# Two query and key jobs of a retention layer ahead of the layer norm that feeds them

## Chip, cores and metric

One core of a Trainium2 chip. The metric is the device time of one execution in microseconds (us). Five engines take part: TensorE (PE, matrix products; PEld in the profile is its weight load), VectorE (DVE), ScalarE (ACT), GpSimd (POOL) and SyncE (SP, which here only issues loads).

## What is computed

Two transformer blocks over 256 positions of 2048 values. The place of the change is the passage from the first layer of the second block (attention, then a layer norm) to its second layer (retention):

```python
def layer_norm(x, gain, bias):
    x32 = x.astype(jnp.float32)
    mu = jnp.mean(x32, axis=-1, keepdims=True)
    var = jnp.mean(jnp.square(x32 - mu), axis=-1, keepdims=True)
    y = (x32 - mu) * lax.rsqrt(var + LN_EPS)
    return (y * gain.astype(jnp.float32) + bias.astype(jnp.float32)).astype(x.dtype)
...
def retention_mixer(h, w_in, decay_exp, w_out, cos, sin):
    B, S, _ = h.shape
    proj = h @ w_in
    q, k, v, g = jnp.split(proj, [R_QK_WIDTH, 2 * R_QK_WIDTH, 2 * R_QK_WIDTH + R_V_WIDTH], axis=-1)
    q = apply_rope(q.reshape(B, S, R_HEADS, R_QK_DIM), cos, sin)
    k = apply_rope(k.reshape(B, S, R_HEADS, R_QK_DIM), cos, sin) * (R_QK_DIM ** -0.5)
...
def second_block(x, attn_w_in, ...):
    ...
        x = layer_norm(ALPHA * x + y, ln_gain[i], ln_bias[i])
```

So with s = ALPHA·x + (attention output), the retention layer multiplies norm(s) by its weights. There are 8 heads of 256 query and key values and 512 values.

## The kernel before

All activations are kept transposed: 16 tiles of 128 features by 256 positions, each as a pair of a rounded part (hi, columns 0 to 255) and what the rounding left (lo, columns 256 to 511). A weight unit of 128x1024 values is loaded by SP as `wf`, rounded by ACT to `wh` (L375), and DVE makes the rest, `wl` = `wf` − `wh` (L388). A product is wh·[hi lo] (512 columns, L450) plus wl·hi (256 columns, L451): a pair. Jobs whose result is not transposed use three 512-wide matmuls (L473 to L475). `next_unit` asks for `wh` three units ahead and for `wl` two units ahead, four buffers of each; a unit lasts 8 pairs.

The order of jobs is written by `plan()`, and all matmuls stand on PE in that order. Everything else is written as Python generators, which `Sched` moves on by one step each time that the matmuls written so far make another 650 ns (`S.adv(325)` per pair); a generator's `yield n` leaves n such steps. Each engine works through its own queue in the order written. So a vector operation stands in its engine's queue between the weight splits where the generator put it, and a split written behind an operation that waits, waits with it.

Stage d ends with four jobs ao (`mm` = 0 to 3), 64 pairs each: the attention output projection, four tiles of 128 features a job. The last two weight units of each job are taken together, tile by tile (`tail=2`), so that the tiles of a job end 8 matmuls apart. `ev_res` adds a finished tile (the hi and lo halves of its PSUM bank, L1375 and L1377) to `xr[k]`, which holds ALPHA·x. The class `LN` gathers the statistics meanwhile: the sum of the first 8 tiles, `lnc`, gives a preliminary mean; once mm=1 has ended, `shift` subtracts it from all 16 tiles (L1296), and `stat` makes a square on ACT (L1320) and two running sums on POOL (L1321, L1323). In mm=3 the weights' last two units come from extra buffers (`alt`), and its 512-wide matmuls are written as two 256-wide ones (`one`, L447 and L448), so that the lo part doesn't need a column of its own to add up. Sums over features are one-column matmuls with a vector of ones (L1342); tiles 14 and 15 have their own. `finish` computes mean and 1/sigma by 13 small DVE operations (L1349 to L499), spreads both over the partitions by two matmuls with diagonals (`lpb` L1358, `lpn` L1366), and `apply0` makes the 16 normed tiles `x3` (named xB): scaling on POOL (L1642), shift on DVE (L1643), gain and bias on ACT (L1646) and on POOL or ACT (L1648, L1650), lo part on DVE (L1654).

Stage e reads `x3`: rqk(0) (query and key of head 0, four tiles, 64 pairs), rv(0) (values), rqk(1,0), rqk(1,2), rv(1), and so on. `task_rope(h)` rotates query and key of a head (L1752 to L1771); rope(0) begins when rqk(0) has ended. `decay` computes the retention decays in 16-column operations on DVE and a logarithm on ACT, during mm=1.

Of the kernel before, what the change touches and what calls it, by code (L numbers as in the profile page):

```python
# [18 lines left out]
P = 128  # L19
# [17 lines left out]
def plan():  # L37
# [72 lines left out]
    for h in range(8):  # L110
        if h == 0:
            job("e", "T", allk, rt(256 * h) + rt(2048 + 256 * h), 2, ("rqk", h, 0))
        else:
            job("e", "T", allk, rt(256 * h), 4, ("rqk", h, 0))
            job("e", "T", allk, rt(2048 + 256 * h), 4, ("rqk", h, 2))
        job("e", "N", allk, [(w, 4096 + 512 * h + ar(512))], 2, ("rv", h))
# [219 lines left out]
def body(tc, a, out, stop=None, dbg=None):  # L336
# [26 lines left out]
    def prefetch(to, alt=None):  # L363

        to = min(len(us), to)
        while pos["sp"] < to:
# [3 lines left out]
            if not raw:  # L370
                if alt is None:
                    wh[q] = pw.tile([P, 1024], F32R, name="wh", tag="wh", bufs=4)
                else:
                    wh[q] = alt.tile([P, 1024], F32R, name="wh", tag="wh", bufs=2)
                ACT.activation(wh[q][:, :n], wf[q][:, :n], AF.Copy)  # L375
            pos["sp"] += 1
        low(to if alt else to - LAG, alt)

    def low(to, alt=None):
        while pos["lo"] < to:  # L380
            q = pos["lo"]
            st, o, n, raw = us[q]
            if not raw:
                if alt is None:
                    wl[q] = pw.tile([P, 1024], F32R, name="wl", tag="wl", bufs=4)
                else:
                    wl[q] = alt.tile([P, 1024], F32R, name="wl", tag="wl", bufs=2)
# [4 lines left out]
    def next_unit(hold=False, alt=None):  # L392
        u = pos["u"]
        if alt is not None:
            low(pos["sp"])
            prefetch(u + SA + 1, alt)
        elif not hold:
# [19 lines left out]
    def job_T(j, xs, evac, tail=1, alt=None, raw=None, one=False):  # L417
# [6 lines left out]
        for c in range(nch - tail + 1):  # L424
            w, ks = {}, []
            for cc in range(c, nch if c == nch - tail else c + 1):
                k0 = cc * kc
                kn = min(kc, K - k0)
                h, l = next_unit(tail > 1 and cc == nch - 1, alt if tail > 1 and cc >= nch - 2 else None)
# [10 lines left out]
            for n, (m, kk) in enumerate(order):  # L440
# [4 lines left out]
                cs = slice(m * P, m * P + P)  # L445
                if one:
# [791 lines left out]

    x2 = XS(S)
    for h in range(2):  # L1240
        act = XS(S, HFF)
        while jq[0]["tag"][0] == "gu":
# [15 lines left out]
    class LN:  # L1258
        tag = "m"

        def __init__(self, pool, x, pair):
# [4 lines left out]
            self.task = None  # L1266
            self.x, self.pair = x, pair
# [20 lines left out]

        def shift(self):
# [3 lines left out]
            ACT.activation(self.c, pb[:, :T], AF.Copy, scale=1.0 / (8 * P))  # L1293
# [75 lines left out]
    def ev_res(ln, mm):  # L1369
        def f(m, p):  # L1370
            k = 4 * mm + m
            S.drain(ln.tpre)
            if k >= 8:
                S.drain(ln.task)
# [581 lines left out]
```

## Time and profile before

| | us |
|---|---|
| median of 3 runs (2297.22 to 2302.93) | 2300.92 |
| the profiled execution | 2303.65 |
| its span in the profile | 2301.9 |
| PE busy in the span | 2265.1 |
| DVE, ACT, POOL busy in the span | 1522.9, 1126.2, 396.2 |
| mm=3 of ao, first to last matmul | 31.41 |
| end of ao to the first matmul of rqk(0) | 9.08 |

The span runs from the first to the last instruction that the profiler saw; the execution's own time has what lies around it as well. PE is busy all the time but for a few places, so the time line of those places, the wait that ended last there, and the granted clock of the stretch are what to read. A granted clock of 1.00 is TensorE's upper level, 2.4 GHz, 0.50 its lower one, 1.2 GHz.

### The profile page before, as it was taken

What the parts mean: (1) busy time and instruction counts of PE and PEld (TensorE: products, weight loads), DVE (VectorE), ACT (ScalarE), POOL (GpSimd) and SP (SyncE); (2) the same over time, 40 slices, a digit from 0 to 9 for tenths busy, and PEclk for the clock granted to TensorE, in tenths of its full rate; (3) what the DMA queues carried; (4) which work ended last, traced back from release to release, by engine and by line L of the source; (5) the groups of instructions that cost most, each with busy time, mean ns of one, the idle gap of its engine ahead of it and who ended that gap; (6) DMA issues with size and microseconds to landing.
All of it is one profiled execution on the core that took longest, in us unless ns stands there. A gap on an engine that the chain in (4) does not pass through costs nothing.

```text
span 2301.9 us, 32643 instructions
## 1 busy us (share of the span) xinstructions
PE 2265.1 (98%) x12407; PEld 1949.7 (85%) x12407; DVE 1522.9 (66%) x2334; ACT 1126.2 (49%) x1642; POOL 396.2 (17%) x369
## 2 busy tenths in 40 slices
PE   8999999999999999999999999999999999999998
PEld 7977878888888888888888888888888888888886
DVE  6666697755555555555558898777676676766554
ACT  5457545554443444454445556454444544445442
POOL 2224341111110011110012222650000000001120
PEclk9999999999999999999999999989999999999998
DMA  7643355566665566656565454444555655556553
GB/s 246 233 147 119 111 186 189 183 192 192 192 193 191 181 191 191 194 188 193 191 191 175 150 157 152 156 166 161 185 169 174 186 165 183 168 173 217 188 182 119
DMA packets 113757, 409.82 MB, mean 178 GB/s; under 512 B 12816, under 2 KB 13072, under 8 KB 113342
## 3 DMA queue, kind: packets, MB, share of 16 engines
q1 hardware_dynamic: 111456, 399.75, 54.2%
q0 software_dynamic: 1424, 6.86, 0.9%
q8 instruction: 97, 1.59, 0.3%
q10 hardware_dynamic: 720, 1.13, 0.1%
q14 instruction: 60, 0.49, 0.1%
HBM read 405.57 MB, written 4.21 MB: 178 GB/s over the span
## 4 chain that ended last, share of the span: by engine, by line
PE 83%; DVE 6%; POOL 2%; issue 1%; ACT 1%; DMA 0%; DVEq 0%; POOLq 0%; ACTq 0%
PE st L450 37%; PE st L451 19%; PE st L473 7%; PE st L474 7%; PE st L475 7%; DVE wl L388 2%; PE mO L1808 1%; POOL xr L1296 1%; PE mA L853 1%; PE mS L1781 0%; PE st L1924 0%; POOL lny L1648 0%; PE mO L834 0%; POOL xr L1642 0%; PE mT L1826 0%
## 5 line engine op out<-in xcount | busy, mean ns | idle before, releaser
L388 DVE TENSOR_TENSOR wl<-wf,wh 128x1024 fp32r<-128x1024 f32 (+1 forms) x750 | 953.2, 1280 | 300.7 <-ACT wh L375 299.4
L375 ACT ACTIVATE wh<-wf 128x1024 fp32r<-128x1024 f32 (+1 forms) x750 | 789.5, 1055 | 696.8 <-PE st L450 397.3
L450 PE MATMUL st<-xA,wh 128*128 128x512 f32 x1952 | 690.4, 397 | 8.0 <-DVE xA L513 6.8
L451 PE MATMUL st<-xA,wl 128*128 128x256 f32 x2016 | 567.8, 282 | 2.6 <-DVE wl L388 2.6
L450 PE MATMUL st<-xB,wh 128*128 128x512 f32 x1536 | 548.8, 401 | 6.0 <-DVE evs L662 2.8
L450 PEld LDWEIGHTS st<-xA,wh 128*128 128x128 f32 x1952 | 367.5, 188 | 89.2 <-DVE xA L513 6.8
L451 PE MATMUL st<-xB,wl 128*128 128x256 f32 x1536 | 432.6, 282 | 0.0
L451 PEld LDWEIGHTS st<-xA,wl 128*128 128x128 f32 x2016 | 384.3, 191 | 3.8 <-DVE wl L388 3.6
L450 PEld LDWEIGHTS st<-xB,wh 128*128 128x128 f32 x1536 | 290.5, 189 | 76.3 <-DVE xB L1654 4.3
L451 PEld LDWEIGHTS st<-xB,wl 128*128 128x128 f32 x1536 | 292.3, 190 | 1.1
L450 PE MATMUL st<-act,wh 128*128 128x512 f32 x704 | 244.1, 392 | 0.0
L451 PE MATMUL st<-act,wl 128*128 128x256 f32 x704 | 197.4, 280 | 0.0
L474 PE MATMUL st<-wl,xB 128*128 128x512 f32 x448 | 175.0, 391 | 1.1 <-DVE wl L388 1.1
L473 PE MATMUL st<-wh,xB 128*128 128x512 f32 x448 | 175.5, 392 | 0.0
L475 PE MATMUL st<-wh,xB 128*128 128x512 f32 x448 | 174.7, 390 | 0.0
L450 PEld LDWEIGHTS st<-act,wh 128*128 128x128 f32 x704 | 131.8, 187 | 28.5
L662 DVE TENSOR_TENSOR evs<-st,evt 128x256 f32<-128x256 f32 x110 | 46.1, 423 | 144.1 <-ACT evt L660 143.8
L451 PEld LDWEIGHTS st<-act,wl 128*128 128x128 f32 x704 | 133.4, 189 | 0.0
L473 PE MATMUL st<-wh,xA 128*128 128x512 f32 (+2 forms) x320 | 122.7, 384 | 0.0
L474 PE MATMUL st<-wl,xA 128*128 128x512 f32 (+2 forms) x320 | 118.5, 370 | 0.5 <-DVE wl L388 0.5
L475 PE MATMUL st<-wh,xA 128*128 128x512 f32 (+2 forms) x320 | 118.4, 370 | 0.0
L1209 POOL TENSOR_TENSOR evs<-evs,R 128x256 f32<-128x256 f32 x44 | 32.4, 737 | 476.8 <-DVE evs L662 476.8
(444 smaller groups left out, 2509.3 us busy)
## 6 DMA issues: line engine op xcount, KB each, us to landing
wf<-in_w_c SPq DMA_DIRECT2D x264, 512.0 KB, 4.2
wf<-in_w_e SPq DMA_DIRECT2D x256, 512.0 KB, 3.7
wf<-in_w_d SPq DMA_DIRECT2D x112, 512.0 KB, 3.7
wf<-in_w_a SPq DMA_DIRECT2D x84, 512.0 KB, 3.6
wf<-in_w_b SPq DMA_DIRECT2D x32, 512.0 KB, 4.1
xr<-in_xT SPq DMA_DIRECT2D x16, 256.0 KB, 5.7
wf<-in_w_a SPq DMA_DIRECT2D x5, 420.0 KB, 4.2
dr<-d POOLq DMA_DIRECT2D x1, 2048.0 KB, 9.7
```

The lines of the kernel that those rows point to most:

```text
L375: ACT.activation(wh[q][:, :n], wf[q][:, :n], AF.Copy)
L388: V.tensor_tensor(wl[q][:, :n], wf[q][:, :n], wh[q][:, :n].bitcast(F32), OP.subtract)
L450: PE.matmul(ps[m], hv[:, cs], x, start=kk == 0, stop=False)
L451: PE.matmul(ps[m][:, :T], lv[:, cs], x[:, :T], start=False, stop=kk == K - 1)
L473: PE.matmul(p, xh, h[:, o:o + n], start=kk == 0, stop=False)
L474: PE.matmul(p, xh, l[:, o:o + n], start=False, stop=False)
L475: PE.matmul(p, xl, h[:, o:o + n], start=False, stop=kk == K - 1)
L662: V.tensor_tensor(s, p[:, :T], t, OP.add)
L853: PE.matmul(pv[:, y, :], qT[i // 2][64 * g:64 * g + 64, i % 2, tt * P:tt * P + P], kT[64 * g:64 * g + 64, b, 0:W], start=True, stop=True)
L1209: G.tensor_tensor(s, s, R2, OP.mult)
L1296: (V if k % 3 == 2 else G).tensor_tensor(xr[k], xr[k], self.c, OP.subtract)
L1808: PE.matmul(po, l[:, st_, o], r_[:, st_], start=i == 0, stop=i == 5)
```

## The change

The norm is linear in s but for its two numbers per position, r = 1/sigma and c = −mean/sigma: norm(s)·W = r·(W·(g s)) + c·(W·g) + W·b, with gain g and bias b. The first two jobs behind ao, rqk(0) and now rqk(1,0), which is moved ahead of rv(0), read new tiles `xg`: the hi and lo parts of g·s without the norm, and four columns between them that hold gain and bias (each hi and lo). Their triples (260, 256, 258 columns) so give W·(g s), W·g and W·b at once, and `ev_first` applies r and c to the finished tiles. `xg` is made by `gain` as soon as the statistics of a tile are written. The norm's sums and broadcasts (`norm0`) are steps of the scheduler among these jobs, `apply0` follows them, and all later jobs read `x3` as before. The preliminary mean comes from the first 4 tiles (`NS`), its subtraction begins with mm=1. The special forms of mm=3 (`alt`, `one`) are not used there, tiles 14 and 15 go through the running sums. The opening of the next stage's pools, the load of the rotation's table and rope(0) go to a function, `phase4`, called when the first half of rv(0) has ended; rope(h) follows rope(h−1). `decay` runs in the second half of the first block's FFN.

```diff
@@ plan
+            if h > 1:
+                job("e", "T", allk, rt(256 * h), 4, ("rqk", h, 0))
             job("e", "T", allk, rt(2048 + 256 * h), 4, ("rqk", h, 2))
+        if h == 0:
+            job("e", "T", allk, rt(256), 4, ("rqk", 1, 0))
@@ job_T
+                if ext:
+                    PE.matmul(ps[m][:, :T + 4], hv[:, cs], x[:, :T + 4], start=kk == 0, stop=False)
+                    PE.matmul(ps[m][:, :T], hv[:, cs], x[:, T + 4:2 * T + 4], start=False, stop=False)
+                    PE.matmul(ps[m][:, :T + 2], lv[:, cs], x[:, :T + 2], start=False, stop=kk == K - 1)
+                    if kk == K - 1:
+                        evac(m, ps[m])
+                    S.adv(340)
+                    continue
@@ LN
+        NS = 4
...
         def shift(self):
-            yield 6
+            yield 5
...
-            for k in [*range(8, 16), *range(8)]:
-                (V if k % 3 == 2 else G).tensor_tensor(xr[k], xr[k], self.c, OP.subtract)
-                if k < 8:
+            n = 0
+            for k in [*range(self.NS, 16), *range(self.NS)]:
+                (V if n % 3 == 2 else G).tensor_tensor(xr[k], xr[k], self.c, OP.subtract)
+                n += 1
+                yield 1
+                if k < self.NS:
+                    S.add(self.stat(k))
                     yield 2
-                    yield from self.stat(k)
...
         def stat(self, k):
+            yield 2
...
+            elif k < 14 or self.done:
                 sq = self.base.tile([P, T], F32, name="lnt", tag="lnt", bufs=3)
                 ACT.activation(sq, xr[k], AF.Square)
                 G.tensor_tensor(self.s, self.s, xr[k], OP.add)
                 yield 1
                 (G if k < 12 else V).tensor_tensor(self.q, self.q, sq, OP.add)
...
+            if self.done:
+                yield 1
+                yield from self.done(k)
@@ finish
+            yield 1
             rsqrt(r[:, 0:2], v, None, None, 2)
+            yield 1
...
                 if z == 2:
+                    if self.done:
+                        yield 2
                     PE.matmul(pb[:, :T], ones, dg[:, :T], start=True, stop=True)
...
+            if self.done:
+                yield 2
             pn = self.pp.tile([P, 512], F32, name="lpn", tag=self.tag)
@@ new: the un-normed tiles, the norm among the jobs
+    def gain(k):
+
+        x = q3.tile([P, 528], F32R, name="xg", tag=f"xg{k}")
+        g = lng[0][:, k:k + 1]
+        ACT.activation(x[:, :T], xr[k], AF.Copy, scale=g)
+        G.tensor_copy(x[:, T:T + 4], cgb[:, k])
+        yield 2
+        V.scalar_tensor_tensor(x[:, T + 4:2 * T + 4], xr[k], g, x[:, :T].bitcast(F32), OP.mult, OP.subtract)
+        xg.t[k] = x
+
+    def gain_by(k):
+        xg.by[k] = S.add(gain(k))
+        if k == 15:
+            tap.append(S.add(norm0()))
+            tap.append(S.add(apply0()))
+        yield 1
...
+    def norm0():
+
+        yield 4
+        ln0.head()
+        ln0.sums(ln0.s, ln0.q, True)
         yield 1
+        yield from ln0.finish()
@@ apply0
+        yield tap[0]
+        rm = ln0.rm
...
-            yield 1 if k < 8 else 2
-
-    tap = S.add(apply0())
+            yield 2 + (k % 3 > 0)
+
+    ln0.begin()
+    for mm in range(1, 4):
+        job_T(take(), og, ev_res(ln0, mm), 2)
...
@@ the jobs' results
+    def ev_first(h, m, p):
+
+        w, s = m // 2, m % 2
+        if s == 0:
+            qkr[(h, w)] = xa_tile("qkr", (P, 2, T))
+        S.drain(tap[0])
+        gb = small(2)
+        V.tensor_reduce(gb, p[:, T:T + 4].rearrange("p (a b) -> p b a", a=2), AX.X, OP.add)
+        q = qkr[(h, w)][:, s]
+        V.tensor_tensor(q, p[:, :T], ln0.rm[1], OP.mult)
+        V.scalar_tensor_tensor(q, ln0.rm[2], gb[:, 0:1], q, OP.mult, OP.add)
+        ACT.activation(q, q, AF.Identity, bias=gb[:, 1:2])
...
+    for h in range(2):
+        job_T(take(), xg, lambda m, p: ev_first(h, m, p), ext=True)
...
+            if (h, tt) == (0, 0):
+                phase4()
```

PE's queue at the end of ao, before: sums between the last pairs, the two broadcasts (`lpb`, `lpn`), then rqk(0) on normed tiles (xB); `pcs` is the PSUM bank of the sums.

```order
L451 MATMUL st<-xA,wl 128x256
L1342 MATMUL pcs<-ones,lns 128x1 x2
L1342 MATMUL pcs<-ones,lnq 128x1 x2
L447 MATMUL st<-xA,wh 128x256
L448 MATMUL st<-xA,wh 128x256
L451 MATMUL st<-xA,wl 128x256
L1342 MATMUL pcs<-ones,xr 128x1 x2
L1342 MATMUL pcs<-ones,lnu 128x1 x2
L1342 MATMUL pcs<-ones,xr 128x1 x2
L1342 MATMUL pcs<-ones,lnu 128x1 x2
L1358 MATMUL lpb<-lndg,ones 128x256
L1366 MATMUL lpn<-lndg,ones 128x256
```

The same place of PE's queue after the change: the last of the nine triples between ao's last pair and the sums, the sums, and the first triple of the ten that stand ahead of `lpb`.

```order
L441 MATMUL st<-xg,wh 128x260
L442 MATMUL st<-xg,wh 128x256
L443 MATMUL st<-xg,wl 128x258
L1359 MATMUL pcs<-deps,ones 128x1 x2
L1393 MATMUL pcs<-ones,lns 128x1 x2
L1393 MATMUL pcs<-ones,lnq 128x1 x2
L441 MATMUL st<-xg,wh 128x260
L442 MATMUL st<-xg,wh 128x256
L443 MATMUL st<-xg,wl 128x258
```

Nothing of the norm is ahead of the first triple any more; nine triples are ahead of the sums, ten more ahead of `lpb`, and three more ahead of `lpn`.

DVE's queue there, before, from the last weight splits of ao to the norm's first small operation (the numbers behind the names tell buffers apart).

```order
L388 TENSOR_TENSOR wl_14528<-wf_14408,wh_14526 128x1024
L388 TENSOR_TENSOR wl_14534<-wf_14438,wh_14532 128x1024
L1375 TENSOR_TENSOR xr_13733<-st_14329,xr_13733 128x256
L1323 TENSOR_TENSOR lnq_13542<-lnq_13542,lnt_14554 128x256
L1375 TENSOR_TENSOR xr_13733<-st_14330,xr_13733 128x256
L1323 TENSOR_TENSOR lnq_13542<-lnq_13542,lnt_14571 128x256
L1375 TENSOR_TENSOR xr_13761<-st_14331,xr_13761 128x256
L1375 TENSOR_TENSOR xr_13761<-st_14332,xr_13761 128x256
L1349 TENSOR_SCALAR sm_14614<-pcs_14356 128x2
```

DVE's queue there after the change; `xg` is the lo part of an un-normed tile (L1651), L385 a weight split.

```order
L1434 TENSOR_TENSOR xr_13808<-st_14364,xr_13808 128x256
L1651 SCALAR_TENSOR_TENSOR xg_14574<-xr_13780,vec_72,xg_14574 128x256
L1372 TENSOR_TENSOR lnq_13589<-lnq_13589,lnt_14581 128x256
L1372 TENSOR_TENSOR lnq_13589<-lnq_13589,lnt_14586 128x256
L1651 SCALAR_TENSOR_TENSOR xg_14589<-xr_13780,vec_72,xg_14589 128x256
L385 TENSOR_TENSOR wl_14605<-wf_14438,wh_14522 128x1024
L385 TENSOR_TENSOR wl_14607<-wf_14460,wh_14601 128x1024
L1651 SCALAR_TENSOR_TENSOR xg_14594<-xr_13808,vec_72,xg_14594 128x256
L1651 SCALAR_TENSOR_TENSOR xg_14614<-xr_13808,vec_72,xg_14614 128x256
L385 TENSOR_TENSOR wl_14642<-wf_14482,wh_14603 128x1024
L1400 TENSOR_SCALAR sm_14662<-pcs_14649 128x2
```

The first job's second and third weight units (wl_14605, wl_14607) are now split behind the last tile's additions, its statistics and one or two `xg` parts. Before, the first job's second and third units (wl_14528, wl_14534) were split ahead of the last four tiles' additions.

## Rows read from the trace of the kernel before

**Rows 1.** Page, sections 1 (busy) and 5 (costliest groups): busy, mean ns, idle before.

```profile
PE 2265.1 (98%) x12407; PEld 1949.7 (85%) x12407; DVE 1522.9 (66%) x2334; ACT 1126.2 (49%) x1642; POOL 396.2 (17%) x369
...
L375 ACT ACTIVATE wh<-wf 128x1024 fp32r<-128x1024 f32 (+1 forms) x750 | 789.5, 1055 | 696.8 <-PE st L450 397.3
```

**Rows 2.** Windows: length, busy of PE, PEld, DVE, ACT, POOL, granted clock, DMA.

```profile
900.00:970.00 70.00, 70.00 (x406) 61.83 (x405) 39.75 (x51) 34.87 (x52) 10.88 (x14) 1.00 0.60 187
...
1483.72:1515.13 31.41, 27.53 (x207) 26.84 (x205) 18.71 (x22) 13.82 (x21) 18.86 (x20) 0.89 0.56 185
...
1493.26:1499.82 6.56, 5.61 (x24) 5.31 (x25) 6.56 (x4) 3.09 (x4) 6.56 (x5) 0.50 0.45 142
...
1515.13:1524.21 9.08, 3.92 (x22) 2.93 (x21) 5.55 (x23) 3.69 (x7) 2.48 (x4) 0.60 0.01 2
...
1516.89:1527.13 10.24, 5.08 (x14) 3.42 (x13) 6.53 (x24) 4.41 (x8) 5.40 (x8) 0.50 0.01 2
...
1524.21:1560.00 35.79, 34.84 (x173) 28.77 (x174) 30.30 (x48) 23.93 (x39) 22.13 (x23) 0.96 0.44 148
```

**Rows 3.** Time line, norm and rqk(0): start, length, engine, line, operation, [idle <-releaser].

```profile
1513.88 0.50 PE L1342 MATMUL pcs<-ones,lns 128*128 128x1 f32 x4
...
1517.01 0.16 DVE L1349 TENSOR_SCALAR sm<-pcs 128x2 f32<-128x2 f32 x1 [1.25 <-PE pcs L1342]
...
1520.01 1.22 PE L1358 MATMUL lpb<-lndg,ones 128*128 128x256 f32 x2 [3.04 <-ACT lndg L1361]
...
1524.21 0.80 PE L450 MATMUL st<-xB,wh 128*128 128x512 f32 x1 [2.12 <-DVE xB L1654]
...
1528.10 0.28 PE L451 MATMUL st<-xB,wl 128*128 128x256 f32 x1
...
1531.28 0.28 PE L451 MATMUL st<-xB,wl 128*128 128x256 f32 x1
```

**Rows 4.** Time line, mm=3 of ao.

```profile
1490.36 1.03 ACT L1320 ACTIVATE lnt<-xr 128x256 f32<-128x256 f32 x3 [1.78 <-POOL xr L1296]
...
1493.26 0.58 PE L447 MATMUL st<-xA,wh 128*128 128x256 f32 x1 [2.77 <-ACT wh L375]
...
1503.08 0.28 PE L447 MATMUL st<-xA,wh 128*128 128x256 f32 x1
...
1503.44 0.28 PE L447 MATMUL st<-xA,wh 128*128 128x256 f32 x1
```

**Rows 5.** Waits of PE: total us, times, longest.

```profile
PE st L450 <- DVE xB L1654: 2.6, 3, 2.1
```

**Rows 6.** Time line, values jobs rv(0) and rv(1).

```profile
1558.27 0.50 PE L474 MATMUL st<-wl,xB 128*128 128x512 f32 x1 [0.51 <-DVE wl L388]
...
1561.88 0.50 PE L474 MATMUL st<-wl,xB 128*128 128x512 f32 x1 [0.60 <-DVE wl L388]
...
1606.46 1.22 DVE L388 TENSOR_TENSOR wl<-wf,wh 128x1024 fp32r<-128x1024 f32 x1
...
1608.74 0.39 PE L474 MATMUL st<-wl,xB 128*128 128x512 f32 x1
```

**Rows 7.** DVE by line and form, 1400 to 1600 us: busy, mean ns, idle.

```profile
L388 DVE TENSOR_TENSOR wl<-wf,wh 128x1024 fp32r<-128x1024 f32 x59 | 78.4, 1351 | 18.4 <-ACT wh L375 18.3
...
L1654 DVE TENSOR_TENSOR xB<-lny,xB 128x256 fp32r<-128x256 f32 x16 | 9.9, 621 | 2.1 <-POOL lny L1648 1.9
...
L1643 DVE TENSOR_TENSOR xr<-xr,lpn 128x256 f32<-128x256 f32 x16 | 6.5, 409 | 0.1
```

**Rows 8.** Time line, rqk(0) beside `apply0`.

```profile
1529.25 1.76 DVE L388 TENSOR_TENSOR wl<-wf,wh 128x1024 fp32r<-128x1024 f32 x1
...
1533.17 1.78 POOL L1648 TENSOR_SCALAR lny<-xr,vec 128x256 f32<-128x256 f32 x1
...
1533.38 1.21 DVE L388 TENSOR_TENSOR wl<-wf,wh 128x1024 fp32r<-128x1024 f32 x1
...
1534.98 0.95 DVE L1654 TENSOR_TENSOR xB<-lny,xB 128x256 fp32r<-128x256 f32 x1
```

More of the change, by code (lines that the diff above doesn't have):

```diff
@@ L1237, in ev_dn, with decay @@
         return f
+    def decay():
+        ne, fr, u, t, z = [small(16) for _ in range(5)]
+        nei = small(16, I32)
+        V.tensor_copy(nei, dexp)
+        V.tensor_copy(ne, nei)
+        V.tensor_tensor(fr, ne, dexp, OP.subtract)
+        V.tensor_scalar(fr, fr, math.log(2.0), None, OP.mult)
+        V.tensor_scalar(u, fr, 1.0 / 9, 1.0, OP.mult, OP.add)
+        for q in range(8, 0, -1):
+            V.tensor_tensor(u, u, fr, OP.mult)
+            V.tensor_scalar(u, u, 1.0 / q, 1.0, OP.mult, OP.add)
+            yield 4
+        V.tensor_scalar(nei, ne, -8388608.0, 127.0 * 8388608.0, OP.mult, OP.add)
+        V.tensor_tensor(u, u, nei.bitcast(F32), OP.mult)
+        V.tensor_scalar(t, u, -1.0, 2.0, OP.mult, OP.add)
+        V.reciprocal(t, t)
+        V.tensor_tensor(t, t, u, OP.mult)
+        V.tensor_tensor(z, t, t, OP.mult)
+        yield 4
+        V.tensor_scalar(ne, z, 1.0 / 9, 1.0 / 7, OP.mult, OP.add)
+        for q in (5, 3, 1):
+            V.tensor_tensor(ne, ne, z, OP.mult)
+            V.tensor_scalar(ne, ne, 1.0 / q, None, OP.add)
+            yield 4
+        V.scalar_tensor_tensor(ne, ne, -2.0, t, OP.mult, OP.mult)
+        V.tensor_scalar(t, u, -1.0, 1.0, OP.mult, OP.add)
+        ACT.activation(t, t, AF.Ln)
+        yield 6
+        V.tensor_scalar(z, u, 0.25, None, OP.is_lt)
+        V.tensor_tensor(ne, ne, t, OP.subtract)
+        V.tensor_tensor(ne, ne, z, OP.mult)
+        V.tensor_tensor(lgd, ne, t, OP.add)
     x2 = XS(S)
@@ L1241, in body @@
         act = XS(S, HFF)
+        if h:
+            S.add(decay())
         while jq[0]["tag"][0] == "gu":
@@ L1323, in stat @@
                 (G if k < 12 else V).tensor_tensor(self.q, self.q, sq, OP.add)
-                if k == 11:
-                    self.ps = self.pp.tile([P, 512], F32, name="pcs", tag=self.tag)
-                    for tt in range(2):
-                        PE.matmul(self.ps[:, 2 + tt:3 + tt], ones, deps, start=tt == 0, stop=False,
-                                  skip_group_check=True)
+                if self.done:
+                    pass
+                elif k == 11:
+                    self.head()
                 elif k == 13:
@@ L1629, in body @@
-    S.add(decay())
-    for mm in range(1, 4):
-        job_T(take(), og, ev_res(ln0, mm), 2, q3 if mm == 3 else None, one=mm == 3)
-    S.drain_all()
-    rm = ln0.finish()
-    x3 = XS(S)
+    cgb = q3.tile([P, 16, 4], F32R, name="cgb")
+    for z, v in enumerate((lng[0], lnb[0])):
+        ACT.activation(cgb[:, :, z], v, AF.Copy)
+        V.tensor_tensor(cgb[:, :, 2 + z], v, cgb[:, :, z].bitcast(F32), OP.subtract)
+    tap = []
+    def norm0():
+        yield 4
+        ln0.head()
+        ln0.sums(ln0.s, ln0.q, True)
+        yield 1
+        yield from ln0.finish()
@@ L1747, in task_rope @@
     def task_rope(h):
+        if h == 0:
+            yield 6
+        else:
+            yield tRo[h - 1]
         xs_ = [qkr.pop((h, w)) for w in range(2)]
```

150 lines of the change are left out of this document (58 added, 92 removed).

## The prediction

> **What bounds the kernel now.** Read first the page's line of busy times: TensorE (PE) is busy for 2265.1 us, 98% of the span [rows 1]. A change can only pay where PE stands still or runs slowly, so I looked next at PE's waits, at stretches of the time line with the granted clock, and at the time line itself where the two jobs of the change stand. There PE loses time in two places that lie next to each other.
>
> The first is the last quarter of the attention output projection (ao, mm=3), 31.41 us long [rows 2]. It holds 64 products of a 512-wide and a 256-wide matmul; nine such pairs take 1531.28 − 1528.10 = 3.18 us, 0.353 us each [rows 3], so the stage needs 22.6 us. What is lost there begins with one wait: VectorE (DVE) and ScalarE (ACT) are not full, but ACT's split of the next weights stands in its queue behind a square that waits for GpSimd (POOL), and PE gets its weights 2.77 us late [rows 4]. PE then runs from 1493.26 to 1499.82 with a granted clock of 0.50, the 1.2 GHz level, and idles for 6.56 − 5.61 = 0.95 us more of it [rows 2].
>
> The second is the norm. Nothing can be multiplied between ao's end at 1515.13 and the first normed tile at 1524.21: 9.08 us, in which the chain sums, 13 small DVE operations, two broadcasts, first tile runs alone [rows 2, 3]. The clock goes to 0.50 again, from 1516.89 to 1527.13 [rows 2], so 2.9 us of the next job run at the lower level too.
>
> **What the change takes away.** (1) The stage mm=3: 31.41 − 22.6 = 8.8 us. Part of it is the wait and the slow clock, part are the sums in the middle of the stage, part the 512-wide matmul written as two 256-wide ones, which is now one again. The POOL work behind the wait does not vanish: it starts one quarter earlier (the mean shift comes from 4 tiles, not 8), so the 8.8 is only gained if it is not late elsewhere (rival A). (2) The norm gap, since the two jobs that follow now read tiles without the norm: 9.1 us. (3) The low clock behind it: 2.9 us at half speed, 1.4 us. (4) Further waits on normed tiles, 2.6 − 2.1 = 0.5 us [rows 5]. (5) The two waits of the first values job on weights, 0.51 + 0.60 = 1.1 us [rows 6], since the rotation that fills DVE there starts later. Sum 20.9.
>
> **What it adds for certain.** The sums and broadcasts of the norm now stand between the matmuls: twelve one-column matmuls in three groups of four, 0.50 us a group by its row [rows 3], the next one starting before the former's end, so 1.2 us (at most 1.5); lpb and lpn took 1.22 us for two instructions of one kind at the low clock [rows 3], so about 0.5 each at the full one, 1.0. The triples of 260, 256 and 258 columns: three 256-wide matmuls take 1503.44 − 1503.08 = 0.36 us [rows 4], by columns 0.36 × 774/768 = 0.3628; less 0.353, times 96, 0.9 us. Sum 3.1; what is left is 17.8.
>
> **What it adds as waits.** No row of before shows these; each is bounded.
> N1, at the switch. The lo part of the second weight unit of the first un-normed job stands on DVE behind the last tile's work: two adds of 0.41 [rows 7], two statistics adds and two gain subtractions. For these four the nearest rows are 0.41 (L1643) and 0.621 (L1654) [rows 7]: I take the mean 0.52, together 2.9, and the split itself 1.21 [rows 8] makes 4.1; PE needs it 8 × 0.36 + 0.24 = 3.1 us after ao's end. Wait 1.0, with the slower value 1.4, so 1.2; ends 0 and 3 (a stretched split and an add, as in rows 8).
> N2, at lpb. The sums come after 9 triples (3.3 us), N1 (1.2) and 1.2 of their own: at 5.7. DVE then does a weight split (1.21) or starts at once; the chain took 1520.01 − 1517.01 = 3.0 us [rows 3], and its last diagonal on ACT may stand behind a split of 1.055 us [rows 1]. So lpb can go at 8.7 to 11.0 us; PE gets there 10 triples on, at 9.3. The wait is 0 to 1.7. Since DVE and ACT have a split in that stretch, I take 1.4, and 0.2 for lpn: 1.6; upper end 3.
> N3, DVE while x3 is made. From the norm (about 12.6 us after ao's end) to the last tile, paced at 1.73 us a tile (650 ns times 2.67 steps, 16 tiles, some 49 us after ao's end), 36.4 us pass. DVE must do 6.5 us of adds, 9.9 of subtractions [rows 7], 12.8 weight splits (a unit in 2.85 us) of 1.351 [rows 7], 17.3, and six evictions with the norm, three operations of some 0.33 in the mean (two of them as L1643, one of two columns), 6.0. That is 39.7, or 3.3 too many. The lead of a split before its use has been as small as 1608.74 − 1607.68 = 1.06 us without a wait [rows 6], so PE would feel 2.3 (splits at 1.21: 0.4 at most; upper end 5, with splits near 1.5).
> Sum of waits 5.1 (0 to 11).
>
> **What costs nothing.** The 45 small operations for the decay go from the attention part to the second FFN half, where DVE is busy 39.75 of 70.00 us and ACT 34.87 [rows 2] and no other work is late; in a fuller stretch they would cost at most 3.0 / 13 = 0.23 us each, as the small ones of the norm do [rows 3]. The 16 gain copies on ACT and POOL and 16 subtractions on DVE fall on the ao stages, as the squares did; DVE was busy 18.71 of 31.41 us there [rows 2]. The same weights are loaded by as many DMAs, those of one job earlier, and nothing else is queued on SP there. The small c4 load on POOL's queue moves by one job, to where the same rotation waits for it. If that rotation and the next head's come close together, the DVE lead of 1.06 us in the second values job is the reserve.
>
> **The sum.** 17.8 − 5.1 = 12.7 us. It is made on the profiled execution, 2303.65 us (span 2301.9): 2290.95. The median of the runs is 2.73 lower than that execution, 2300.92, so 2288.2, forecast 2288.
>
> **A rule that speaks against it.** What the rows show: a weight split takes 1.76 us at 1529.25 and 1.21 at 1533.38, a subtraction 0.95 at 1534.98 where the mean is 0.621; POOL's instruction beside the 1.21 one takes 1.78 [rows 7, 8]. So the two engines slow each other, by turns. The Trainium skill, "SBUF — State Buffer", section "Who interferes with whom", says that a DVE instruction with two SBUF inputs contends with a GpSimd one that reads SBUF, through a port pair held exclusively. The trace agrees in that one of the two is long in each case; by the rule alone every subtraction and split of N3 would be held, which is the mechanism of rival C; the saving of 12.7 is that of the mean durations in the trace, −6.1 that of the held ones.
>
> **The rivals.**
> A, the POOL wait only moves. POOL does the mean shift of 16 tiles and the statistics of 8 in the second quarter. If it is late there, the same square holds the same split: 2.77 + 0.95, and 6.56 us at the low clock, another 3.3. The saving falls from 12.7 to 5.7: 2295. For it: POOL is busy 18.86 of 31.41 us in mm=3 [rows 2], and the work is as much as before. Against it: all subtractions now come ahead of the squares of the tiles of that quarter, which was not so before.
> B, everything added is hidden. DVE does its small work in gaps; saving 17.8: 2283. Against it: DVE has 30.30 us of work in 35.79 already before [rows 2].
> C, slower. In the un-normed jobs and the first values job, DVE collides with POOL's 16 scalings and gain operations: subtractions at 0.95 (15.2), splits at 1.76 (22.5), 6.5 and 6.0 as above, 50.2 us in 36.4. PE waits 12.7, 10.4 more than in N3, and each of two late splits costs a stretch at the low clock of 3.3 to 5.1 (half of 6.56 and 10.24) [rows 2]: 8.4 more. 12.7 − 18.8 = −6.1: 2307. It decides once a split takes some 1.6 and a subtraction 0.8 in the mean there. Against it: the mean of 59 splits around this place, POOL's work included, was 1.351 [rows 7].
> D, it doesn't do what it says: the first triple waits for the last un-normed tile or for the norm, the gap stays and with it most of the 12.1; 2299.
>
> **How the numbers follow.** Forecast as worked (saving 8 to 17): 0.62. A: 0.18. B: 0.10. C: 0.06. D: 0.04. A range of 2281 to 2296 holds the forecast, B and most of A, with waits from none to the upper ends (17.8 − 11 = 6.8: 2294) and two us for the scatter of runs. A measurement of this kernel tells 0.3%, 6.9 us, from no change. Faster than that: forecast, B, and a part of A (0.07), 0.79. Within: the rest of A, D, 0.15. Slower: C, 0.06.
>
> **What the profile would show.** mm=3 some 23 us long at clock 1.00, no wait of PE on wh; no gap behind ao's last matmul, instead triples at once; one wait of 1 to 2 us on wl in the first three us, one of similar size at lpb, some of 0.2 to 1 us on wl until x3 is ready; no 0.50 between 1480 and 1600. Wrong would be: squares ahead of wh with a long wait in mm=1 or mm=2, splits of 1.7 us in a row, a clock of 0.50 in the un-normed jobs, or a late split in the second values job.

## The result

The changed kernel takes 2286.93 us in the median of 20 runs (2282.6 to 2299.73), the kernel before 2302.12 us in the median of the 20 beside it. One run of the kernel before, of 7951.97 us, counts as slow and is left out of the ratio. The ratio of the others, which is not that of the two medians, is 0.9939, with a 95% interval of 0.9925 to 0.9954: 14.0 us less, between 10.6 and 17.3. The forecast was 2288, 12.7 us less, in a range of 2281 to 2296.

The runs of both kernels lie in two groups some 13 us apart: 14 of after at 2282.60 to 2287.94 and 6 at 2297.73 to 2299.73; of before 18 at 2297.22 to 2304.01 and one at 2316.28. The medians of the two lower groups, 2301.95 and 2285.95, differ by 16.0 us.

The time is best compared over the passage that the change touches: from ao's first matmul to the first one behind rv(1), both read from the time line. It holds the same matrix products in every kernel of this text, but for small ones: of the eight transposes of head 0 (`mT`) that lie in it before, four stand just behind its end in after (and in all kernels below but early_stats, early_stats_decay and one_job), where they take 0.36 us.

| kernel | passage, us | ao's start to rqk(0)'s | from there on |
|---|---|---|---|
| before | 211.87 (1411.70 to 1623.58) | 112.51 | 99.37 |
| after | 194.90 (1424.19 to 1619.09) | 94.19 | 100.71 |
| difference | −17.0 | −18.3 | +1.3 |

The profiled execution of after took 2299.29 us, 4.4 us less than that of before and not 17, because its feed-forward part, where the change does not matter for PE, was 13.8 us longer; the last section tells of that. It is about what lies between the two groups of runs.

The page of after, its line of busy times [rows 1], and from its list of PE's waits the one that is new in the passage (waits in all, times, longest):

```profile
PE 2271.2 (99%) x12423; PEld 1946.4 (85%) x12423; DVE 1534.2 (67%) x2368; ACT 1134.2 (49%) x1661; POOL 406.4 (18%) x384
...
PE st L443 <- DVE wl L385: 1.2, 1, 1.2
```

The waits for `wh` (2.77), for the diagonals ahead of `lpb` (3.04) and for the normed tiles (2.6) are gone from that list [rows 3 to 5], and so are those of rv(0) [rows 6]. Windows of after (length; busy time of PE, PEld, DVE, ACT, POOL; granted clock): mm=3, the stretch at the lower clock, and the stretch in which the normed tiles are made.

```profile
1496.19:1518.37 22.18, 22.18 (x130) 19.56 (x129) 16.45 (x22) 11.06 (x17) 8.13 (x13) 1.00 0.58 191
1525.43:1528.85 3.42, 3.42 (x18) 3.42 (x18) 2.97 (x16) 0.54 (x2) 0.00 (x0) 0.51 0.93 316
1531.00:1566.00 35.00, 35.00 (x261) 33.56 (x260) 33.55 (x61) 27.31 (x42) 24.73 (x25) 1.00 0.52 164
```

mm=3 takes 22.2 us at a clock of 1.00, where it took 31.41 at 0.89 [rows 2]. The lower level comes back for 3.4 us. While the normed tiles are made, DVE is busy 33.55 of 35.00 us, and PE all of it. The time line of after at ao's end:

```profile
1518.25 0.28 PE L453 MATMUL st<-xA,wl 128*128 128x256 f32 x1
1518.37 0.28 PE L441 MATMUL st<-xg,wh 128*128 128x260 f32 x1
...
1519.77 1.50 DVE L1372 TENSOR_TENSOR lnq<-lnq,lnt 128x256 f32<-128x256 f32 x2
...
1521.58 2.35 DVE L385 TENSOR_TENSOR wl<-wf,wh 128x1024 fp32r<-128x1024 f32 x2
...
1522.85 0.39 PE L443 MATMUL st<-xg,wl 128*128 128x258 f32 x1 [1.22 <-DVE wl L385]
...
1529.51 0.60 PE L1413 MATMUL lpb<-lndg,ones 128*128 128x256 f32 x2
```

ao's last matmul starts at 1518.25 and the first un-normed triple 0.12 us later: the gap of 9.08 us [rows 2] is closed. The ninth triple finds its `wl` missing for 1.22 us, since DVE begins the split at 1521.58, behind the statistics; `lpb` (L1413) does not wait.

### The profile page after: what moved, and what is told of

Its sections match the earlier page's. It is cut to its first block, busy times and chain, and to the rows that moved or that the text cites. A ratio compares the mean times of both kernels' runs of the same rounds, so it can differ in the third digit from the quotient of the medians.

```text
span 2297.5 us, 32746 instructions
## 1 busy us (share of the span) xinstructions
PE 2271.2 (99%) x12423; PEld 1946.4 (85%) x12423; DVE 1534.2 (67%) x2368; ACT 1134.2 (49%) x1661; POOL 406.4 (18%) x384
## 4 chain that ended last, share of the span: by engine, by line
PE 87%; DVE 5%; ACT 1%; issue 1%; POOL 1%; POOLq 0%; DVEq 0%; ACTq 0%
PE st L452 39%; PE st L453 20%; PE st L475 7%; PE st L477 7%; PE st L476 7%; DVE wl L385 2%; PE mO L1889 1%; PE mA L855 1%; PE mS L1862 0%; PE st L443 0%; PE st L441 0%; PE st L442 0%; PE st L2004 0%; PE mO L836 0%; PE mT L1907 0%
## 5 line engine op out<-in xcount | busy, mean ns | idle before, releaser
L385 DVE TENSOR_TENSOR wl<-wf,wh 128x1024 fp32r<-128x1024 f32 (+1 forms) x750 | 954.8, 1282 | 287.8 <-ACT wh L375 287.1
L452 PE MATMUL st<-xA,wh 128*128 128x512 f32 x2016 | 722.6, 402 | 8.1 <-DVE xA L515 6.8
L452 PE MATMUL st<-xB,wh 128*128 128x512 f32 x1440 | 511.4, 399 | 2.4 <-DVE evs L664 1.8
L452 PEld LDWEIGHTS st<-xA,wh 128*128 128x128 f32 x2016 | 380.9, 189 | 100.9 <-DVE xA L515 6.7
L453 PE MATMUL st<-xB,wl 128*128 128x256 f32 x1440 | 404.3, 281 | 0.0
L452 PEld LDWEIGHTS st<-xB,wh 128*128 128x128 f32 x1440 | 271.3, 188 | 67.0 <-DVE evs L664 2.5
L453 PEld LDWEIGHTS st<-xB,wl 128*128 128x128 f32 x1440 | 272.4, 189 | 1.0
L452 PE MATMUL st<-act,wh 128*128 128x512 f32 x704 | 248.8, 399 | 0.0
```

The source lines that it names most:

```text
L385: V.tensor_tensor(wl[q][:, :n], wf[q][:, :n], wh[q][:, :n].bitcast(F32), OP.subtract)
L452: PE.matmul(ps[m], hv[:, cs], x, start=kk == 0, stop=False)
L453: PE.matmul(ps[m][:, :T], lv[:, cs], x[:, :T], start=False, stop=kk == K - 1)
```

## The experiments

The passage of each, in the order of this section; each is one profiled execution. Medians of all runs (2 to 10 of each kernel) stand beside it, with the spread of 13.8 us in them that the last section describes. How far one execution can be trusted shows in ao: after and the seven kernels from split_first on have the same matrix products and the same statistics there, and it took 94.12 to 95.38 us. A difference of about 1 us in the passage means something only where a wait or a stretch of the clock accounts for it. The expectations count "after" as 194.9 and "before" as 211.9.

| kernel | passage | ao's start to rqk(0)'s | from there on | median |
|---|---|---|---|---|
| early_stats | 210.78 | 111.24 | 99.54 | 2300.34 |
| decay_back | 202.61 | 101.88 | 100.73 | 2294.13 |
| early_stats_decay | 203.07 | 104.73 | 98.34 | 2292.72 |
| late_stats | 205.71 | 105.08 | 100.62 | 2295.09 |
| split_first | 194.46 | 94.79 | 99.67 | 2285.24 |
| lpb_later | 193.96 | 95.38 | 98.58 | 2283.59 |
| fast_apply | 202.01 | 94.79 | 107.22 | 2293.14 |
| one_job | 197.09 | 95.31 | 101.78 | 2287.47 |
| pool_all | 196.13 | 94.83 | 101.31 | 2286.19 |
| pool_none | 196.40 | 94.12 | 102.27 | 2285.40 |
| lpb_later_act | 193.70 | 94.67 | 99.03 | 2283.48 |

### Early statistics alone (early_stats)

```diff
--- the kernel before
+        NS = 4
-            for k in [*range(8, 16), *range(8)]:
+            for k in [*range(self.NS, 16), *range(self.NS)]:
...
     S.add(decay())
+    ln0.begin()
     for mm in range(1, 4):
```

> The kernel before with only the statistics begun a quarter earlier (mean shift from 4 tiles, at the start of mm=1), all else as before: norm in its old place, special forms of mm=3 kept. Measure: the passage from ao's first matmul to the last of rv(1), 211.9 us in before, 194.9 in after. Theory (what held ACT was POOL's backlog, and the backlog is gone by mm=3): no wait on wh in mm=3 and no 0.50 clock there, passage 211.9 - 7.0 = 204.9. Rival (the wait only moves to mm=1 or mm=2): a wait on wh there and a passage of about 211 to 212.

The passage was 210.78, 1.1 us less than before. No wait for `wh` was left in mm=3, as the theory said. But PE now waits 6.8 us for `wl`; 1.5 us of it lie at the start of the FFN, as in every kernel here, the other three waits in mm=1. So neither theory had it: the lost time moved, and not onto ACT. The list of PE's waits, and the time line of POOL and DVE there:

```profile
PE st L451 <- DVE wl L388: 6.8, 4, 2.2
```

```profile
1454.86 7.97 POOL L1302 TENSOR_TENSOR xr<-xr,lnc 128x256 f32<-128x256 f32 x10 [2.40 <-ACT lnc L1298]
...
1454.70 0.17 DVE L1625 TENSOR_SCALAR sm<-sm 128x16 f32<-128x16 f32 x1
1454.91 0.72 DVE L1624 TENSOR_TENSOR sm<-sm 128x16 f32<-128x16 f32 x1
1455.67 0.65 DVE L1625 TENSOR_SCALAR sm<-sm 128x16 f32<-128x16 f32 x1
...
1459.03 1.82 DVE L388 TENSOR_TENSOR wl<-wf,wh 128x1024 fp32r<-128x1024 f32 x1
```

The 16-column operations are the decay's. One that runs before POOL starts its ten subtractions takes 0.17 us, those beside them 0.65 to 0.72, and the split at 1459.03 stands behind thirteen of them. The ten subtractions take 7.97 us, 0.8 each: a small operation lasts nearly as long as the POOL instruction beside it. The rule that the prediction weighed is seen here where the DVE instruction is short. The Trainium skill, "SBUF — State Buffer", section "Who interferes with whom", names as the one cause of contention a port pair shared by the two engines, an exclusive lock, and says that a DVE instruction with two SBUF inputs contends there with a GpSimd one that reads SBUF. For the operations with two inputs in SBUF (L1624) the rows agree: 0.72 us, beside POOL instructions of 0.8. Those with one such input (L1625) are nearly as long, 0.65, and no run here shows why.

### The decay back in mm=1 (decay_back)

```diff
--- the changed kernel
         act = XS(S, HFF)
-        if h:
-            S.add(decay())
...
+    S.add(decay())
     ln0.begin()
     for mm in range(1, 4):
```

> The changed kernel with the decay computed during mm=1 of ao again, with its old steps, all else as changed. Theory (from the run with early statistics alone: a 16-column operation on DVE takes 0.65 to 0.72 us beside POOL's subtractions, 0.17 otherwise, and the weight splits wait behind them): waits on wl of about 5 us in all in mm=1 and the start of mm=2, passage 194.9 + 5 = 200. Rival (what the prediction says of this part, 45 operations of at most 0.23 us in a place with room): passage 195 to 196.

202.61, 7.7 us more than after. The list of PE's waits has, for this kernel:

```profile
PE st L453 <- DVE wl L385: 7.7, 5, 2.5
```

After has 1.5 us of waits for `wl` on that line, the one at the start of the FFN. All of the loss lies before ao's end (101.88 against 94.19); from there on the two kernels are alike to 0.02 us. 6.6 us of it lie in mm=1, where the decay runs (29.66 us against 23.02, from last matmul to last matmul); 1.0 lies in mm=2, with a wait of 0.66 us on `wl` that lpb_later, one_job and pool_all have as well, so that it is hardly the decay's. The prediction's claim for this edit is refuted as a statement on the place that the operations left; it holds for the place to which they went.

### Early statistics, with the decay moved (early_stats_decay)

```diff
--- the kernel before
+        NS = 4
...
         act = XS(S, HFF)
+        if h:
+            S.add(decay())
...
-    S.add(decay())
+    ln0.begin()
     for mm in range(1, 4):
```

> The kernel before with the early statistics and with the decay in the second half of the FFN; no un-normed jobs, special forms of mm=3 kept. Theory (the early statistics did take away 7 us in mm=3, and the decay gave 5.6 back): passage 210.8 - 5.6 = 205.2, no wait on wl in mm=1, norm gap as before. Rival (the splits wait in mm=1 or mm=2 for POOL's work anyway): passage 208 or more.

203.07, 8.8 us less than before. The window of mm=3 (from its first matmul to the sums), and what the list of PE's waits still has of the norm:

```profile
1480.98:1504.44 23.46, 23.46 (x198) 23.46 (x197) 16.04 (x17) 10.50 (x14) 6.53 (x6) 1.00 0.66 224
```

```profile
PE lpb L1411 <- ACT lndg L1414: 3.0, 1, 3.0
...
PE st L450 <- DVE xB L1677: 2.6, 3, 2.1
```

mm=3 runs at full clock, 23.5 us even with its special forms, and the waits of the norm gap are as before. Against early_stats this is −7.7 us. That decay_back gave 7.7 too, from the other side, is in part luck: mm=1 differs by 6.5 us here (29.48 and 23.00) and by 6.6 there, and the rest lies in other places, here behind ao's end. So beside the early statistics the decay in mm=1 costs about 6.5 us. Of the 17.0 us, 8.8 have nothing to do with un-normed jobs; these give the other 8.2, together with the dropped special forms and the 0.36 us of transposes behind the passage's end.

### Late statistics (late_stats)

```diff
--- the changed kernel
-        NS = 4
+        NS = 8
...
+            if k == self.NS - 1:
+                self.begin()
...
-    ln0.begin()
     for mm in range(1, 4):
```

> The changed kernel with the statistics as late as before (mean shift from 8 tiles, begun after mm=1), all else as changed. Theory: POOL's backlog holds ACT again in mm=3 or at the switch, a wait on wh of 2 to 4 us and a stretch at the lower clock, passage 194.9 + 7 = 202 or more, since POOL's copies for the un-normed tiles come on top. Rival (the earlier start is not what removed the wait, the dropped special forms of mm=3 are): passage 195 to 196.

205.71, 10.8 us more than after. From the list of PE's waits, and ACT's time line:

```profile
PE st L452 <- ACT wh L375: 6.6, 2, 6.2
```

```profile
1503.00 0.42 ACT L1371 ACTIVATE lnt<-xr 128x256 f32<-128x256 f32 x1 [5.07 <-POOL lnq L1374]
...
1507.32 1.99 ACT L375 ACTIVATE wh<-wf 128x1024 fp32r<-128x1024 f32 x2
```

ACT idles 5.07 us until POOL has freed a buffer of the squares (L1374), then does squares and un-normed tiles, and comes to the weights at 1507.32; PE starts again at 1508.42. The stall of before [rows 4] is back and larger. The rival, that dropping the special forms of mm=3 had removed it, falls. The wait, 6.25 us, is longer than the 2 to 4 that the theory gave.

### The split written first (split_first), and lpb later (lpb_later)

```diff
--- the changed kernel
+        if ahead:
+            low(u + 3)
...
-        job_T(take(), og, ev_res(ln0, mm), 2)
+        job_T(take(), og, ev_res(ln0, mm), 2, ahead=mm == 3)
```

> The changed kernel with the lo split of the second weight unit of the first un-normed job written ahead of the last four tiles' operations on DVE. Theory (that split behind the last tile's work costs a wait of 1.22 us and a stretch of 3.4 us at the lower clock, 1.7 us): passage 194.9 - 2.9 = 192.0, lpb without a wait. Rival (lpb did not wait only because PE was late itself): DVE's chain of small operations starts near 6.2 us after ao's end and ends near 9.2, PE is at lpb at 8.0; a wait of about 1.2 us at lpb with a low clock behind it, passage 193.5 to 195.

194.46; from ao's end on 99.67, 1.0 us less than after. The wait on the split and the lower clock are gone, and the rival's wait at `lpb` is there (time line of split_first):

```profile
1513.30 0.28 PE L445 MATMUL st<-xg,wl 128*128 128x258 f32 x1
1514.69 0.48 PE L1415 MATMUL lpb<-lndg,ones 128*128 128x256 f32 x1 [1.12 <-ACT lndg L1418]
```

So `lpb` did not wait in after only because PE itself came later. The rival's low clock behind that wait did not follow. The un-normed jobs took 38.15 us against 39.67, so 1.5 us were gained; rv(0) gave 0.5 back (22.27 against 21.81), as its splits, with leads of 0.05 us, came just too late. The second kernel adds one edit to the first:

```diff
--- split_first
                     if self.done:
-                        yield 2
+                        yield 4
```

> The run with the split written first, and lpb two steps (some 3.8 triples, 1.3 us) later among the matmuls, so that PE meets it when its diagonals are there. Theory (N2 is a wait of PE for a chain whose end is set by DVE): no wait at lpb, the rest unmoved, passage 194.5 - 1.1 = 193.4. Rival (the normed tiles then come later, and the values job, where the lead of a split was 0.05 us, pays): passage 194 to 195, with waits on wl in rv(0).

From ao's end on 98.58, 1.1 us less than split_first: the wait is gone, as the theory had it to 0.1. The passage is 193.96 and not 193.4, as ao was 0.6 us longer than in split_first (a wait of 0.66 us on `wl` in mm=2, 0.15 there). The rival is right in one point: rv(0) has a wait of 0.23 us on `wl`. The un-normed jobs, now without a wait and at full clock, took 37.00 us: in after N1 and the clock behind it cost 39.67 − 37.00 = 2.7 us.

### The pace of the normed tiles (fast_apply)

```diff
--- the changed kernel
-            yield 2 + (k % 3 > 0)
+            yield 1 if k < 8 else 2
```

> The changed kernel with the normed tiles made at the old pace (a step apart for the first eight, two steps for the others, instead of 2.67 in the mean). Theory N3 (DVE is full while x3 is made: more per microsecond cannot be taken): 16 tiles in some 16 us, DVE would need about 6.5 + 9.9 + 9 + 2 = 27 us there, late by 11 against leads of 3 to 5: waits on wl of 4 us or more with a lower clock, passage 199 to 203. Rival (leads are large enough, the pace doesn't matter): passage 194 to 196.

202.01, 7.1 us more than after, 6.5 of them behind ao's end. From the list of PE's waits, and the time line at the longest one:

```profile
PE st L443 <- DVE wl L385: 5.7, 5, 3.7
```

```profile
1543.45 0.39 PE L443 MATMUL st<-xg,wl 128*128 128x258 f32 x1 [3.67 <-DVE wl L385]
...
1544.05 0.42 PE L443 MATMUL st<-xg,wl 128*128 128x258 f32 x1
```

Four waits on `wl` while the tiles are made (the fifth is that at the switch), the longest 3.67 us, with matmuls of 0.42 us behind it, where the full level has 0.28: the clock fell. N3 is a real limit: DVE has no room for so much faster a pace.

### One un-normed job instead of two (one_job)

```diff
--- the changed kernel
-    for h in range(2):
+    for h in range(1):
         job_T(take(), xg, lambda m, p: ev_first(h, m, p), ext=True)
```

and rqk(1,0) back behind rv(0) in `plan`.

> The changed kernel with only rqk(0) un-normed; rqk(1,0) reads normed tiles in its old place behind rv(0). Theory (the normed tiles are paced so that the last is there some 46 us after ao's end, and rv(0) needs it at 48.8, the first at 28): no wait on normed tiles, DVE's lead of 0.3 us in rv(0) is used up by about 1 us, passage 195 to 197. Rival (DVE is full, so a job less of cover is paid): waits on wl or xB in rv(0) of 3 us or more with a lower clock, passage 199 or more.

197.09, 2.2 us more than after, at the theory's upper end. There is no wait in rv(0) at all, 1.1 us of the difference lies in ao (0.67 of it a wait on `wl` in mm=2, in work that is the same in both), and 1.1 behind it. Of that, 0.36 are the four transposes that the passage of after does not hold, and the rest goes with short waits and stretched matmuls in rv(1). One job is enough to hide the norm; the second buys some 0.7 us, which one execution of each does not show for certain.

### POOL's share (pool_all, pool_none), and with the best version (lpb_later_act)

```diff
--- the changed kernel (pool_all; pool_none has k < 0)
-            if k % 2:
+            if k >= 0:
                 G.tensor_scalar(y, xr[k], g, o, OP.mult, OP.add)
```

> The changed kernel with all sixteen gain-and-bias copies for the lo parts of the normed tiles on POOL (before: eight there, eight on ACT). Rival C of the prediction (DVE and POOL hold each other): splits near 1.76 and subtractions near 0.95 us in the mean, DVE needs some 50 us where 36 pass, waits on wl of 10 us and low clocks, passage 205 or more. Theory (what decides is the sum of DVE's work against the time and a lead of 5 us; in the changed kernel splits have 1.51 there, subtractions 0.52): splits up to 1.6, POOL some 9 us longer, passage 196 to 200.

> The changed kernel with all sixteen of these copies on ACT. Theory (POOL's copies stretch DVE's splits beside them, but the lead hides it): splits fall from 1.51 to about 1.4 us, the smallest lead in rv(0) rises from 0.3 us to 1 us or more, passage 194.9 as before within 0.5. Rival (ACT is late with wh instead): a wait on wh or xB, passage 196 or more.

196.13 and 196.40. DVE's splits and subtractions, grouped by line and form while the tiles are made (count, busy us, mean ns), of after, then of pool_all, then of pool_none:

```profile
L385 DVE TENSOR_TENSOR wl<-wf,wh 128x1024 fp32r<-128x1024 f32 x11 | 16.6, 1511 | 0.0
L1707 DVE TENSOR_TENSOR xB<-lny,xB 128x256 fp32r<-128x256 f32 x16 | 8.3, 523 | 0.5 <-POOL lny L1701 0.4
```

```profile
L385 DVE TENSOR_TENSOR wl<-wf,wh 128x1024 fp32r<-128x1024 f32 x11 | 15.1, 1375 | 0.0
L1707 DVE TENSOR_TENSOR xB<-lny,xB 128x256 fp32r<-128x256 f32 x16 | 9.8, 617 | 0.9 <-POOL lny L1701 0.4
```

```profile
L385 DVE TENSOR_TENSOR wl<-wf,wh 128x1024 fp32r<-128x1024 f32 x11 | 15.8, 1432 | 0.3 <-ACT wh L375 0.3
```

With all copies on POOL splits have 1.375 us, with none 1.432, with half 1.511: the share that POOL has of these copies does not set it. In each kernel a split mostly takes either 1.21 or 1.76 us; six of the eleven took the longer time in after, three in pool_all, four in pool_none, so that the means differ by a few splits only. Rival C's trigger (1.6 and 0.8) was not reached with twice the copies on POOL (busy 30.96 of 36 us, 24.73 of 35 in after), and its 205 is refuted. Half of pool_all's 1.2 us lies in ao, half in rv(0).

The theory's time for pool_none was missed, 1.5 us more than after, but this says nothing of the copies. All of it lies in a longer stretch at the lower clock behind the wait at the switch, which is the same wait of 1.21 us as in after, and that stretch differs between kernels with this wait (last section). The smallest lead in rv(0) was 0.59 us, not 1. This window of pool_none answers to the 3.42 us of after:

```profile
1509.40:1516.30 6.90, 6.90 (x33) 6.90 (x34) 5.61 (x20) 1.75 (x3) 0.00 (x0) 0.51 0.62 223
```

> The run with the split first and lpb later, and all sixteen copies on ACT. Theory: both edits work in different places, from ao's end to the end of rv(1) 98.6 us as with lpb later alone, or 0.4 less, since the wait of 0.23 in rv(0) goes; no wait on wl in rv(0). Rival: ACT's queue holds wh, 99.5 or more.

99.03 from ao's end on, 0.45 more than lpb_later: no gain, and rv(0) waits 0.64 us on `wl`. The theory falls here, and the rival's 99.5 was not reached; why rv(0) waits longer is open. Its median (2283.48) and that of lpb_later (2283.59) are alike, and the lowest of all versions; each is some 3 us below the changed kernel's median, of which the passages show 0.9 to 1.2.

## Why the prediction was right, and where it was off

The direction and the two places were right: 8.8 us were forecast for mm=3 and 9.1 for the gap, and the table shows 18.3 us gone up to the start of rqk(0). That 12.7 us came so close to the measured 14.0 is in part luck: compared within the lower group of runs the gain is 16.0 us, and over the passage 17.0, mainly since two of the three waits that were forecast did not come. Point by point:

**(1) mm=3.** 31.41 became 22.2 us (window above) against 22.6 forecast; in split_first, lpb_later, fast_apply, one_job and lpb_later_act it was 22.6. Shown: late_stats brings the stall back, early_stats_decay removes it without the rest of the change. The end of the stall, with the sums' move out of the stage (0.8 us), makes 31.41 − 23.46 = 8.0 us; the dropped special forms, and in part the rhythm of PE, make the rest.

**(2) to (5) the gap and what follows.** The gap is 0. The low clock behind it is replaced by one behind N1, in the un-normed jobs, which the prediction had named as a sign that it was wrong. The waits of 0.5 and 1.1 us are gone.

**Added for certain, 3.1 us.** Sums from 1523.07 to 1524.34, 1.3 us; the first eight triples 1518.37 to 1521.23, 0.358 us each, so 0.5 us for 96 against 0.9; `lpb` and `lpn` 0.4 each against 0.5. About 2.6 in all.

**N1, right in size.** 1.2 forecast, 1.22 measured, for the reason given: the split begins at 1521.58 behind the adds, the statistics and two `xg` parts. What the sum left out is the lower clock behind it: N1 and the clock together cost 2.7 us (lpb_later), so the clock 1.5.

**N2, 1.6 forecast, 0 measured.** The chain is as long as forecast (1525.78 to 1528.71 in after, 2.9 us against 3.0), and it begins behind a split, as taken:

```profile
1524.64 1.22 DVE L385 TENSOR_TENSOR wl<-wf,wh 128x1024 fp32r<-128x1024 f32 x1
1525.78 0.15 DVE L1400 TENSOR_SCALAR sm<-pcs 128x2 f32<-128x2 f32 x1
...
1528.31 0.40 ACT L1416 ACTIVATE lndg<-ident,sm 128x128 f32<-128x128 f32 x1 [4.31 <-DVE sm L501]
```

Three kinds of run tell what the wait depends on. Without N1 (split_first) it is 1.12 us. With N1 and no lower clock behind it (fast_apply, late_stats) it is 0.59:

```profile
1508.90 0.39 PE L443 MATMUL st<-xg,wl 128*128 128x258 f32 x1 [1.21 <-DVE wl L385]
...
1514.82 0.48 PE L1413 MATMUL lpb<-lndg,ones 128*128 128x256 f32 x1 [0.59 <-ACT lndg L1416]
```

```profile
1508.90:1515.41 6.51, 5.92 (x46) 5.66 (x47) 6.06 (x19) 2.20 (x4) 0.00 (x0) 1.00 0.70 239
```

(fast_apply, time line and window.) With both, in after, it is nothing: the diagonals are there at 1528.71, and PE comes to `lpb` at 1529.51, 0.8 us later. So N2 was mis-sized, and what it then cost was paid in advance: delays of PE ahead of a wait shorten it. The prediction let N1 move the sums and PE alike, which left the wait as it was. Counted from ao's end, PE comes to `lpb` 1.5 us later in fast_apply than in split_first, and the diagonals only 1.0 us later.

**N3, 2.3 forecast, 0 measured.** This is the term that was mis-sized most, in two steps. The first is the load. The prediction added up durations, 39.7 us for 36.4. In the window of 35.00 us above, the durations of the same groups add up to 16.6 + 8.3 + 6.6 + 6.3 = 37.8 us (splits, subtractions, adds, evictions), and yet DVE is busy for 33.55 and idle for 1.45, since the records of one operation and the next overlap:

```profile
1531.72 0.42 DVE L1695 TENSOR_TENSOR xr<-xr,lpn 128x256 f32<-128x256 f32 x1 [1.60 <-PE lpn L1423]
1532.06 1.75 DVE L385 TENSOR_TENSOR wl<-wf,wh 128x1024 fp32r<-128x1024 f32 x1
```

The split starts 0.34 us after an add of 0.42. Over the 61 operations of the window this is 4.2 us, more than the 3.3 that the prediction found missing. The durations themselves were off both ways: splits had 1.511 us (1.351 taken), subtractions 0.523 (0.621). The second step is the reserve. It was taken from rv(1), 1.06 us [rows 6], and that was the wrong stage. In the first un-normed job PE first uses a `wl` 4.3 to 6.6 us after it is done (the third to sixth unit), and in rv(0) the smallest lead is 0.3 us (a split done at 1566.16, used at 1566.47). So DVE did fall behind while the tiles were made, and a lead of 5 us absorbed it and was all but used up. fast_apply shows what lies behind: 6.5 us from ao's end on.

**What costs nothing.** The decay's new place cost PE nothing, as said (no wait on `wl` between 450 and 1150 us; the second FFN job, beside which it runs, takes 243.94 us in split_first as in before). The bound of 0.23 us an operation for a fuller stretch was wrong by a factor of three, 0.65 to 0.72: it came from a stretch in which POOL was idle. Without this edit the change gains 9.3 us over the passage, not 17.0 (decay_back). And no price was given to the early statistics meeting the decay in mm=1, the one collision that was real.

**The rivals.** A did not happen; it would have, in another dress (DVE, not ACT), without the decay's move. B came nearest, 17.8 against 17.0 over the passage, though by a different account: N1 with its clock was paid, and small terms came out lower. D is refuted by the closed gap, C by after and pool_all. The rule behind C, by which every split would be held, is borne out for some: six of eleven took 1.76 us and five 1.21 in after.

**The account.** Up to the start of rqk(0) 17.9 us were forecast and 18.3 measured. From there on the terms come to 3.1 + 5.1 − 1.4 − 0.5 − 1.1 = 5.2 us more than before, and 1.3 were measured. Of these 3.9 us, N2 and N3 are 3.9 and the smaller additions 0.5, against 1.5 for the clock behind N1; 0.36 are the transposes that left the passage. The 0.6 that are left lie in small terms that were not told apart, the rhythm of PE (below) perhaps among them.

## What to carry to other kernels

A tile that is scaled and shifted after the product needs no norm before it, and here one such job, not two, already hides a norm chain of 9 us; the statistics must be there earlier, and their work must not meet short vector operations. Waits of one engine that come one after another do not simply add up, and a load on an engine is paid only beyond the lead that its products have at that place: read the lead there, not in a later stage. For the load itself take busy time from a window, not a sum of durations, which counts overlaps twice. When POOL gets work, look for small DVE operations beside it, and move them away.

## What the runs showed of the hardware

**Short DVE operations beside POOL.** 0.17 us became 0.65 to 0.72 at 16 columns, four times as much, while a split of 1.21 became 1.76 beside the normed tiles and 1.82 in early_stats, half as much again.

**A low clock after a short wait.** Seven kernels have the wait of 1.2 us at the switch, in a stretch otherwise full. In five it was followed by 3.4 us (after, decay_back, one_job, pool_all) or 6.9 us (pool_none) at the lower level, beginning 1 to 3 us after the wait; in two (fast_apply, late_stats) it was not, and neither was the wait of 1.1 us at `lpb` in split_first. What decides is open. The price of such a wait so differed by up to 3 us between kernels with the same wait.

**Two rhythms of PE.** Windows of the same 100 us in the FFN, of before and then of after, no wait and full clock in both:

```profile
600.00:700.00 100.00, 100.00 (x579) 88.35 (x578) 55.87 (x72) 47.07 (x64) 11.18 (x14) 1.00 0.61 190
```

```profile
600.00:700.00 100.00, 100.00 (x568) 86.79 (x567) 52.63 (x63) 46.73 (x64) 11.13 (x14) 1.00 0.61 189
```

579 matmuls against 568. In the first, a pair takes 230 and 117 ns, 347 together, each time to within a nanosecond; in the second 236 and 117 in the mean, scattered by 3, together 353. A rhythm holds from the last wait near 440 us to the FFN's end: its second job of 1408 matmuls takes 243.94 or 248.62 us, in all thirteen profiled kernels one or the other, and the whole FFN 13.8 us more in the second. The second rhythm was found in after, early_stats and late_stats, which explains their own times (2299.29, 2314.91, 2310.89) beside their medians; that the upper groups of runs in the section on the result have it too is likely, and no profile shows it for the others. It comes by chance, since the code up to there is the same in early_stats and in before; that it is drawn anew at each wait of PE is argued from the changes of the step near 440 us, not shown. mm=3 of ao shows the same two paces, 22.18 or 22.6 us for 64 pairs. A change of a few microseconds in this kernel is therefore better read from its passage than from the total of one execution, and a change of less than one from neither.
